# Input columns laid out by the host, scales spread by a product with ones, and a first unit whose weights come in row blocks

## The chip, the cores and the metric

The kernel runs on one core of one Trainium2 chip. The time is the device time of one execution in microseconds (us), and of several executions the median counts. The engines are TensorE (PE in the profile, with PEld for its weight loads), VectorE (DVE), ScalarE (ACT), GpSimd (POOL) and SyncE (SP), which only issues transfers here. Each engine works through its own instructions in order and waits at semaphores for the others.

## The reference

One decoder layer on 2048 tokens of 1024 float32 features. The part that the change touches is at the front: the tokens are normalised, multiplied by one large weight matrix, and three groups of four attention heads are cut out of the product.

```python
h = rms_norm(x, norm_w[layer])          # x * rsqrt(mean(x*x) + eps) * norm_w, per token
proj = h @ w_in[layer]                  # 1024 -> 9224 columns
(dn_qkv, dn_z, dn_b, dn_a, swa_q, swa_k, swa_v, swa_z, gates) = jnp.split(proj, split_points, axis=-1)
...                                     # branch A: a chunked gated delta rule
sq = partial_rope(rms_norm(grp(swa_q), q_norm_w[layer][:, None, :]), cos, sin)
sk = partial_rope(rms_norm(grp(swa_k), k_norm_w[layer][:, None, :]), cos, sin)
...                                     # branch B: windowed attention per group and head, merged by softmax sums
x = x + merged @ w_out[layer]
```

All of it is computed in float32 accuracy. Each large product is therefore made of three: both factors are split into a rounded part and the rest, and high by high, high by low and low by high are added up.

## The kernel before, in words

**The normalised input.** The tokens are worked in 16 tiles of 128. The products need a tile with the features on the partitions, so `hh` (rounded part) and `hl` (rest) hold it in 8 blocks of 128 features, in two halves of 4. For each tile t, `x_load` (L95) brings 128 x 1024 inputs, `x_norm` makes the sum of squares on ScalarE (L102) and the scale on GpSimd (L103, and L105 with a power of -1/2), and VectorE multiplies the tile by scale and norm weights in one instruction of 1024 elements (L106). `x_trans` then has TensorE transpose the 8 blocks (L116, products with an identity) into PSUM, from which ScalarE rounds each half into `hh` (L119) and VectorE subtracts it into `hl` (L120).

**The first stage** (`swa`, from the start to about 1044 us) is 12 units, one per head and group, of 16 steps. Step t of a unit multiplies token tile t by 384 weight columns (q, k and v of the head): 24 products of 384 columns (`s_proj`, L176 to L178), two blocks of features at a time, with slots between them. In the slots stand the pieces of an attention tile that is two steps older (`att_slots`): slot 0 transposes its probabilities (L265), slot 1 makes its scores (L249 to L251, VectorE's masking and row maximum L253 and L256, ScalarE's exponential L258), slot 2 multiplies by v (L273, L274) and transposes the q and k of the next one (L231, with L238 and L239 behind it). At the end of a step `s_norm` normalises q and k: ScalarE squares and sums (L191) and copies v (L192), GpSimd makes the scales (L195, L197), VectorE multiplies (L199), and GpSimd rotates (L207 to L210).

**Only in the first unit** are the token tiles made as well: in step t, after slot 1, `x_trans(t + 1)` and `x_norm(t + 2)`. The other units find them ready.

**Weights.** `w384` loads the 1024 x 384 weights of a unit in six pieces (four feature blocks by one of q, k, v; L155), and splits each with ScalarE (L79) and VectorE or GpSimd (L80). For the first unit this stands ahead of step 0; the second unit's pieces are split in steps 14 and 15 of the first, those of the later units one per step from step 6.

**What sets the order.** In this stage the order on TensorE, ScalarE, VectorE and GpSimd is the order in which the code is written; a scheduler places only the transfers, all on the SP queue. A tile of a pool with two or three buffers waits until the reader of an earlier one is done. PSUM has three `mm`, two `tp`, two `sc` and one `po`. After the first stage come the delta rule, its scan, and the last products, which the change leaves as they are.

## Time and profile before

| | us |
|---|---|
| median of 3 runs | 2417.84 |
| lowest, highest | 2412.42, 2421.81 |
| the profiled execution, its own time | 2415.66 |
| its span, first to last instruction | 2413.5 |
| TensorE busy in the span | 2362.7 |
| VectorE, ScalarE, GpSimd busy | 1160.2, 846.1, 835.1 |
| ScalarE's first square (L191) of tile 0 in unit 0 | 26.61 |
| the same of tile 15 in unit 0 | 126.35 |
| the same of tile 0 in unit 1 | 135.32 |

The profiled execution lies 2.18 us under the median of the runs, and 2.16 us of its time lie outside the span. In a row of the timeline stand the start, the duration (for a row that merges several instructions, from the first start to the last end), the engine, the source line, the operation, the tiles written and read, the sizes and the count; in brackets how long the engine had been idle before, and what released it. A matmul's row is longer than its share of the engine, because the next one starts while it drains: the distance of two starts is what one costs.

### The profile page before, as it was taken

To read this page: it belongs to the slowest core of one execution; us is meant where nothing else is said; L and a number is where in the kernel's file an instruction comes from. 1 tells how busy PE (TensorE), PEld (TensorE's weight loads), DVE (VectorE), ACT (ScalarE), POOL (GpSimd) and SP (SyncE) were. 2 spreads that over 40 slices of the span, in tenths; PEclk is the share of its full clock that TensorE was granted. 3 is DMA by queue.
4 is the path that set the end of the run, shared out by engine and by line. 5 is a ranking of instruction groups with operands and counts; after the bars stand their busy time and mean duration, and the time that the engine had idled before them with its cause. 6 is when DMAs were issued, how large, how long until landed. Compare 5 with 4: busy or idle time off the path is not lost.

```text
span 2413.5 us, 40161 instructions
## 1 busy us (share of the span) xinstructions
PE 2362.7 (98%) x13710; PEld 2147.6 (89%) x13710; DVE 1160.2 (48%) x2738; ACT 846.1 (35%) x2985; POOL 835.1 (35%) x1785
## 2 busy tenths in 40 slices
PE   7999999999999999999999999999999999999999
PEld 6999999999999999987777878888888878889998
DVE  4644433243344334343766665999444433454431
ACT  4544443244444333323665662111243313111110
POOL 3533433533343344410533551111133212442441
PEclk9999999999999999999999999999999999999999
DMA  4211101233343344433444443222566655555542
GB/s 139 72 44 35 39 23 50 87 113 97 100 118 104 100 120 115 115 98 101 124 122 120 111 120 114 75 75 71 180 200 192 185 165 156 162 181 157 150 139 75
DMA packets 348819, 274.22 MB, mean 114 GB/s; under 512 B 57864, under 2 KB 317256, under 8 KB 348232
## 3 DMA queue, kind: packets, MB, share of 16 engines
q1 hardware_dynamic: 348616, 271.66, 39.1%
q8 instruction: 109, 1.79, 0.3%
q14 instruction: 94, 0.77, 0.1%
HBM read 167.47 MB, written 104.10 MB: 113 GB/s over the span
## 4 chain that ended last, share of the span: by engine, by line
PE 86%; DMA 4%; DVE 4%; ACT 2%; POOL 2%; issue 1%; SPq 1%; DVEq 0%; ACTq 0%; POOLq 0%
PE mm L176 11%; PE mm L178 11%; PE mm L177 11%; PE mm L413 9%; PE mm L415 8%; PE mm L414 8%; PE mm L903 2%; PE mm L905 2%; PE mm L904 2%; PE mm L886 2%; PE mm L888 2%; PE mm L887 2%; DMA gcb<-gcscr 2%; PE po L274 2%; PE tp L231 2%; PE tp L265 1%
## 5 line engine op out<-in xcount | busy, mean ns | idle before, releaser
L176 PE MATMUL mm<-wh,hh 128*128 128x384 f32 (+1 forms) x1536 | 554.5, 361 | 2.4 <-ACT wh L79 2.4
L177 PE MATMUL mm<-wl,hh 128*128 128x384 f32 (+1 forms) x1536 | 519.4, 338 | 1.8 <-DVE wl L80 1.2
L178 PE MATMUL mm<-wh,hl 128*128 128x384 f32 (+1 forms) x1536 | 520.0, 339 | 0.0
L413 PE MATMUL mm<-hh,wh 128*128 128x512 f32 x1152 | 467.1, 406 | 0.0
L415 PE MATMUL mm<-hh,wl 128*128 128x512 f32 x1152 | 456.0, 396 | 0.0
L414 PE MATMUL mm<-hl,wh 128*128 128x512 f32 x1152 | 452.9, 393 | 0.0
L176 PEld LDWEIGHTS mm<-wh,hh 128*128 128x128 f32 x1536 | 290.4, 189 | 5.3 <-ACT wh L79 3.0
L177 PEld LDWEIGHTS mm<-wl,hh 128*128 128x128 f32 x1536 | 291.3, 190 | 2.5 <-DVE wl L80 1.4
L178 PEld LDWEIGHTS mm<-wh,hl 128*128 128x128 f32 x1536 | 289.7, 189 | 0.0
L415 PEld LDWEIGHTS mm<-hh,wl 128*128 128x128 f32 x1152 | 217.8, 189 | 47.7
L413 PEld LDWEIGHTS mm<-hh,wh 128*128 128x128 f32 x1152 | 217.9, 189 | 43.6
L414 PEld LDWEIGHTS mm<-hl,wh 128*128 128x128 f32 x1152 | 218.1, 189 | 41.9
L80 POOL TENSOR_TENSOR wl<-raw,wh 128x512 fp32r<-128x512 f32 (+1 forms) x75 | 106.9, 1437 | 405.4 <-ACT wh L79 405.0
L199 DVE SCALAR_TENSOR_TENSOR rec<-mm,st,wqk 128x128 f32<-128x128 f32 x256 | 78.1, 347 | 275.2 <-POOL st L197 261.6
L258 ACT ACTIVATE p<-sc,ol 128x128 f32<-128x128 f32 (+1 forms) x192 | 82.0, 427 | 342.8 <-DVE ol L256 310.2
L195 POOL TENSOR_SCALAR st<-st 128x2 f32<-128x2 f32 x192 | 48.8, 254 | 398.1 <-ACT rec L191 269.2
L886 PE MATMUL mm<-oh,hh 128*128 128x256 f32 x512 | 143.7, 281 | 3.0 <-DVE gt L890 2.9
L888 PE MATMUL mm<-oh,hl 128*128 128x256 f32 x512 | 142.9, 279 | 0.0
L887 PE MATMUL mm<-ol,hh 128*128 128x256 f32 x512 | 142.8, 279 | 0.0
L518 DVE SCALAR_TENSOR_TENSOR acc<-xr,cw,acc 128x512 f32<-128x512 f32 x144 | 121.8, 846 | 42.4 <-ACT acc L516 37.8
L197 POOL TENSOR_TENSOR st<-st,mhalf 128x2 f32<-128x2 f32 x192 | 134.7, 702 | 16.0
L191 ACT ACTIVATE rec<-mm 128x128 f32<-128x128 f32 x256 | 68.5, 273 | 160.6 <-PE mm L178 116.1
(240 smaller groups left out, 4346.6 us busy)
## 6 DMA issues: line engine op xcount, KB each, us to landing
raw<-in_w_in_dram SPq DMA_DIRECT2D x144, 256.0 KB, 3.1
rscr<-rec SPq DMA_DIRECT2D x128, 192.0 KB, 1.9
qk<-rscr SPq DMA_DIRECT2D x128, 128.0 KB, 2.3
gscr<-gt SPq DMA_DIRECT2D x64, 256.0 KB, 2.5
gt<-gscr SPq DMA_DIRECT2D x64, 256.0 KB, 3.4
oscr<-ol SPq DMA_DIRECT2D x192, 65.0 KB, 1.9
oc<-oscr SPq DMA_DIRECT2D x16, 780.0 KB, 5.0
rec<-rec SPq DMA_DIRECT2D x16, 768.0 KB, 5.3
```

The costliest lines, as they stand in the source:

```text
L80: eng.tensor_tensor(out=l, in0=raw, in1=h.bitcast(F32), op=ALU.subtract)
L176: nc.tensor.matmul(pr[:, :w], a, wh[:, k, :w], start=(k == 0), stop=False)
L177: nc.tensor.matmul(pr[:, :w], a, wl[:, k, :w], start=False, stop=False)
L178: nc.tensor.matmul(pr[:, :w], b, wh[:, k, :w], start=False, stop=(k == KT - 1))
L197: nc.gpsimd.tensor_tensor(out=st[:, 2:4], in0=st[:, 0:2], in1=self.mhalf[:, 0:2], op=ALU.pow)
L413: nc.tensor.matmul(pr, wh[:, k, :], a, start=(k == 0), stop=False)
L414: nc.tensor.matmul(pr, wh[:, k, :], b, start=False, stop=False)
L415: nc.tensor.matmul(pr, wl[:, k, :], a, start=False, stop=(k == KT - 1))
L518: nc.vector.scalar_tensor_tensor(out=acc, in0=xr[:, j:j + 512], scalar=w[:, j:j + 1], in1=acc, op0=ALU.mult, op1=ALU.add)
L886: nc.tensor.matmul(o, self.wbh[:, k, ms], oh[:, k, :], start=(k == b * 4), stop=False)
L887: nc.tensor.matmul(o, self.wbh[:, k, ms], ol[:, k, :], start=False, stop=False)
L888: nc.tensor.matmul(o, self.wbl[:, k, ms], oh[:, k, :], start=False, stop=(k == b * 4 + 3))
```

## The change

**The input, twice.** The host adds `xcol`, the same inputs with the features of each block on the partitions, and the norm weights as a 128 x 8 table `nwc`. For each token tile both forms are loaded (`x_load`), 512 KB each. The row form is only squared and summed (`x_stat`); GpSimd makes the scale as before and one instruction more, the identity times the scale, a diagonal `dg` of 128 x 128.

**The scale as a row.** `x_rows` multiplies 128 x 128 ones by that diagonal, so that each of 128 rows in PSUM holds the scales of the 128 tokens. `x_scale` multiplies the 8 blocks of `xc` in place, each by its norm weights (a scalar per partition) and by that row: 8 VectorE instructions of 128 elements. `x_high` rounds each half on ScalarE, `x_low` subtracts, the first half on VectorE and the second on GpSimd. The 8 transposes of a tile are gone, and the two PSUM tiles of `mm` that they took; the row takes a `tp`.

**When.** `XCOL` lists which tiles are made in which step of the first unit: one per step, two in steps 4 and 8, the last in step 12. The second unit's weights begin at step 13 with one piece split there, three in step 14 and two in step 15.

**The start.** The first unit's weights come in 8 row blocks of 128 features by q, k and v (`w_first`, 192 KB each), five ahead of the loop, split one by one in turn on VectorE and GpSimd. The transfers of the first `xcol` tile, the identity and the norm weights are issued by ScalarE. 24 products of 256 columns on the zeroed `kq` tile stand first on TensorE (`warm`).

```diff
--- before.py
+++ after.py
@@ -33,6 +33,8 @@
 C_SV = C_SK + 1536
 C_SZ = C_SV + 1536
 C_GT = C_SZ + 512
+
+XCOL = [[1], [2], [3], [4], [5, 6], [7], [8], [9], [10, 11], [12], [13], [14], [15], [], [], []]
 
 
 def dr(ap, off, dims):
@@ -83,42 +85,60 @@
     def x_setup(self, xp):
         nc = self.nc
         self.xp = xp
-        self.xt, self.xn = {}, {}
-        self.x_load(0)
-        self.nwb = xp.tile([P, D], F32, name="nwb", bufs=1)
-        nc.sync.dma_start(self.nwb, dr(self.i["norm_w"], 0, [[0, P], [1, D]]))
-        nc.sync.dma_start(self.ident, self.i["ident"])
-        self.x_norm(0)
-
-    def x_load(self, t):
+        self.xt, self.xc, self.dg = {}, {}, {}
+        self.ones = xp.tile([P, P], F32, name="ones", bufs=1)
+        self.nw = xp.tile([P, KT], F32, name="nw", bufs=1)
+        nc.vector.memset(self.ones, 1.0)
+        self.x_load(0, nc.scalar)
+        nc.scalar.dma_start(self.ident, self.i["ident"])
+        nc.scalar.dma_start(self.nw, self.i["nwc"])
+
+    def x_load(self, t, q=None):
+        nc = self.nc
         self.xt[t] = self.xp.tile([P, D], F32, name="xt", bufs=2)
-        self.nc.sync.dma_start(self.xt[t], dr(self.i["x"], P * t * D, [[D, P], [1, D]]))
-
-    def x_norm(self, t):
+        nc.sync.dma_start(self.xt[t], dr(self.i["x"], P * t * D, [[D, P], [1, D]]))
+        self.xc[t] = self.xp.tile([P, KT, P], F32, name="xc", bufs=2)
+        (q or nc.sync).dma_start(self.xc[t].rearrange("p k c -> p (k c)"), dr(self.i["xcol"], P * t * D, [[D, P], [1, D]]))
+
+    def x_stat(self, t):
         nc = self.nc
         xt = self.xt.pop(t)
         st = self.xp.tile([P, 2], F32, name="xst", bufs=2)
-        xn = self.xn[t] = self.xp.tile([P, D], F32, name="xn", bufs=2)
-        nc.scalar.activation(xn, xt, AF.Square, accum_out=st[:, 0:1])
+        dg = self.dg[t] = self.xp.tile([P, P], F32, name="dg", bufs=2)
+        nc.scalar.activation(xt, xt, AF.Square, accum_out=st[:, 0:1])
         nc.gpsimd.tensor_scalar(out=st[:, 0:1], in0=st[:, 0:1], scalar1=1.0 / D, scalar2=EPS,
                                 op0=ALU.mult, op1=ALU.add)
         nc.gpsimd.tensor_tensor(out=st[:, 1:2], in0=st[:, 0:1], in1=self.mhalf[:, 0:1], op=ALU.pow)
-        nc.vector.scalar_tensor_tensor(out=xn, in0=xt, scalar=st[:, 1:2], in1=self.nwb, op0=ALU.mult, op1=ALU.mult)
-
-    def x_trans(self, t):
-        nc = self.nc
-        xn = self.xn.pop(t)
-        n, c = t // 4, (t % 4) * P
+        nc.gpsimd.tensor_scalar(out=dg, in0=self.ident, scalar1=st[:, 1:2], scalar2=None, op0=ALU.mult)
+
+    def x_rows(self, t):
+        pt = self.ps.tile([P, 512], F32, name="tp", bufs=2)
+        self.nc.tensor.matmul(pt[:, :P], self.ones, self.dg.pop(t), start=True, stop=True)
+        return pt[:, :P]
+
+    def x_scale(self, t, rows, half):
+        xc = self.xc[t]
+        for k in range(half * 4, half * 4 + 4):
+            self.nc.vector.scalar_tensor_tensor(out=xc[:, k, :], in0=xc[:, k, :], scalar=self.nw[:, k:k + 1], in1=rows,
+                                                op0=ALU.mult, op1=ALU.mult)
+
+    def x_high(self, t, half):
+        n, c, ks = t // 4, (t % 4) * P, slice(half * 4, half * 4 + 4)
+        self.nc.scalar.activation(self.hh[:, n, ks, c:c + P], self.xc[t][:, ks, :], AF.Copy)
+
+    def x_low(self, t, half, eng):
+        n, c, ks = t // 4, (t % 4) * P, slice(half * 4, half * 4 + 4)
+        eng.tensor_tensor(out=self.hl[:, n, ks, c:c + P], in0=self.xc[t][:, ks, :], in1=self.hhf[:, n, ks, c:c + P],
+                          op=ALU.subtract)
+
+    def x_col(self, t):
+        rows = self.x_rows(t)
         for half in range(2):
-            pt = self.ps.tile([P, 512], F32, name="mm", bufs=3)
-            for j in range(4):
-                k = half * 4 + j
-                nc.tensor.transpose(pt[:, j * P:(j + 1) * P], xn[:, k * P:(k + 1) * P], self.ident)
-            ks = slice(half * 4, half * 4 + 4)
-            src = pt.rearrange("p (k c) -> p k c", c=P)
-            nc.scalar.activation(self.hh[:, n, ks, c:c + P], src, AF.Copy)
-            nc.vector.tensor_tensor(out=self.hl[:, n, ks, c:c + P], in0=src, in1=self.hhf[:, n, ks, c:c + P],
-                                    op=ALU.subtract)
+            self.x_scale(t, rows, half)
+        for half in range(2):
+            self.x_high(t, half)
+            self.x_low(t, half, (self.nc.vector, self.nc.gpsimd)[half])
+        self.xc.pop(t)
 
 
     def swa_setup(self, sp):
@@ -131,6 +151,34 @@
         self.rope = sp.tile([P, 16, 32], F32, name="rope", bufs=1)
         self.att = []
         self.att_next = 0
+
+    def warm(self, count):
+        pr = self.ps.tile([P, 512], F32, name="mm", bufs=3)
+        for _ in range(count):
+            self.nc.tensor.matmul(pr[:, :256], self.kq[:, 0, 0, :], self.kq[:, 0, 0:2, :].rearrange("p a c -> p (a c)"),
+                                  start=True, stop=True)
+
+    def w_first(self, wp, h, g):
+        nc, i = self.nc, self.i
+        wh = wp[0].tile([P, KT, wp[1]], F32R, name="wh")
+        wl = wp[0].tile([P, KT, wp[1]], F32R, name="wl")
+        self.wqk = self.sp.tile([P, 2, P], F32, name="wqk", bufs=1)
+        raws = []
+
+        def load():
+            k = len(raws)
+            raw = self.rawp.tile([P, 4, P], F32, name="raw")[:, 0:3, :] if k % 5 < 3 else \
+                self.xp.tile([P, 3, P], F32, name="raw0", bufs=2)
+            nc.sync.dma_start(raw, dr(i["w_in"], k * P * NIN + C_SQ + g * 512 + h * P, [[NIN, P], [1536, 3], [1, P]]))
+            raws.append(raw.rearrange("p a c -> p (a c)"))
+
+        def high(k):
+            nc.scalar.activation(wh[:, k, :384], raws[k], AF.Copy)
+
+        def low(k):
+            (nc.gpsimd if k % 2 else nc.vector).tensor_tensor(out=wl[:, k, :384], in0=raws[k],
+                                                              in1=wh[:, k, :384].bitcast(F32), op=ALU.subtract)
+        return (wh, wl, self.wqk), load, high, low
 
     def w384(self, wp, h, g, first=False):
         nc, i = self.nc, self.i
@@ -310,43 +358,66 @@
         nc = self.nc
         step = self.step
         nu = len(units)
-        gen = self.w384(wps[0](), *units[0], first=True)
-        w = {0: next(gen)}
-        for _ in range(3):
-            next(gen)
+        w0, load, high, low = self.w_first(wps[0](), *units[0])
+        w = {0: w0}
+        for _ in range(5):
+            load()
+        self.warm(24)
+        self.x_stat(0)
+        rows = self.x_rows(0)
+        high(0)
+        low(0)
+        self.x_scale(0, rows, 0)
+        high(1)
+        low(1)
+        high(2)
+        self.x_high(0, 0)
+        self.x_scale(0, rows, 1)
+        self.x_low(0, 0, nc.vector)
+        self.x_high(0, 1)
+        self.x_low(0, 1, nc.gpsimd)
+        self.xc.pop(0)
+        low(2)
         self.x_load(1)
+        for k in range(3, 8):
+            if k < 6:
+                load()
+            high(k)
+            low(k)
+            if k == 4:
+                self.x_stat(1)
+        self.x_load(2)
+        for j, nm in enumerate(("q_norm_w", "k_norm_w")):
+            nc.sync.dma_start(w0[2][:, j, :], dr(self.i[nm], units[0][1] * P, [[0, P], [1, P]]))
         nc.sync.dma_start(self.rope, self.i["rope"])
         nc.sync.dma_start(self.mask, self.i["mask"])
-        self.x_trans(0)
-        for _ in gen:
-            pass
-        self.x_norm(1)
         for u in range(nu):
             gen = None
             for t in range(16):
-                if u == 0 and t + 2 < 16:
-                    self.x_load(t + 2)
                 s = dict(h=units[u][0], g=units[u][1], t=t, pr=None, w=w[u])
                 self.s_proj(s, (0, 1))
                 self.att_slots(step, 0)
                 self.s_proj(s, (2, 3))
                 self.att_slots(step, 1)
-                if u == 0 and t < 15:
-                    self.x_trans(t + 1)
-                    if t < 14:
-                        self.x_norm(t + 2)
-                    else:
+                if u == 0:
+                    for c in XCOL[t]:
+                        self.x_col(c)
+                        if c + 2 < 16:
+                            self.x_load(c + 2)
+                        if c + 1 < 16:
+                            self.x_stat(c + 1)
+                    if t == 12:
                         xctx.close()
                 self.s_proj(s, (4, 5))
                 self.att_slots(step, 2)
                 self.s_proj(s, (6, 7))
                 self.s_norm(s)
                 self.att_add(s, step)
-                if u + 1 < nu and t >= (14 if u == 0 else 6):
+                if u + 1 < nu and t >= (13 if u == 0 else 6):
                     if gen is None:
                         gen = self.w384(wps[(u + 1) % 2](), *units[u + 1])
                         w[u + 1] = next(gen)
-                    for _ in range(4 if u == 0 else 1):
+                    for _ in range((2, 3, 3)[t - 13] if u == 0 else 1):
                         next(gen, None)
                 step += 1
         self.step = step
@@ -1048,6 +1119,8 @@
     nc = bacc.Bacc("TRN2", target_bir_lowering=False, num_devices=1)
     data = {name: np.ascontiguousarray(inputs[name]) for name in _INS}
     data.update(consts())
+    data["xcol"] = np.ascontiguousarray(data["x"].reshape(16, P, KT, P).transpose(0, 3, 2, 1)).reshape(T, D)
+    data["nwc"] = np.ascontiguousarray(data["norm_w"].reshape(KT, P).T)
     arrays, ins = {}, {}
     for name, a in data.items():
         arrays[f"in_{name}_dram"] = a
```

The order of VectorE's instructions in a step of the first unit, before, from one subtraction of the k and q tile to the next (`kq` and `qk` are the attention's, `sc` and `ol` the score and its maximum, `xn` and `hl` the token tile):

```order
L239 TENSOR_TENSOR kq<-tp,kq 128x256
L199 SCALAR_TENSOR_TENSOR qk<-mm,st,wqk 128x128 x2
L253 ISA sc,ol<-sc,mask 128x256
L253 ISA ol 128x1
L256 TENSOR_SCALAR ol<-ol 128x1
L120 TENSOR_TENSOR hl<-mm,hh 128x4x128 x2
L106 SCALAR_TENSOR_TENSOR xn<-xt,xst,nwb 128x1024
L276 COPY ol<-po 128x128
```

And now, in the same place (lines are those of the changed kernel; `xc` is the token tile):

```order
L287 TENSOR_TENSOR kq<-tp,kq 128x256
L247 SCALAR_TENSOR_TENSOR qk<-mm,st,wqk 128x128 x2
L301 ISA sc,ol<-sc,mask 128x256
L301 ISA ol 128x1
L304 TENSOR_SCALAR ol<-ol 128x1
L122 SCALAR_TENSOR_TENSOR xc<-xc,nw,tp 128x128 x8
L131 TENSOR_TENSOR hl<-xc,hh 128x4x128
L324 COPY ol<-po 128x128
```

Eight small instructions on `xc` stand where two subtractions and one long multiplication stood; the q and k scaling and the score are still ahead of them.

GpSimd in a step of the first unit, before (`xst` is the token scale, `st` that of q and k):

```order
L103 TENSOR_SCALAR xst<-xst 128x1
L105 TENSOR_TENSOR xst<-xst,mhalf 128x1
L195 TENSOR_SCALAR st<-st 128x2
L197 TENSOR_TENSOR st<-st,mhalf 128x2
L207 TENSOR_TENSOR t_696<-qk,rope 128x64
L208 TENSOR_TENSOR t_697<-qk,rope 128x64
```

And now:

```order
L131 TENSOR_TENSOR hl<-xc,hh 128x4x128
L109 TENSOR_SCALAR xst<-xst 128x1
L111 TENSOR_TENSOR xst<-xst,mhalf 128x1
L112 TENSOR_SCALAR dg<-ident,xst 128x128
L243 TENSOR_SCALAR st<-st 128x2
L245 TENSOR_TENSOR st<-st,mhalf 128x2
```

The subtraction of the second half and the diagonal are new, and both stand ahead of the scale of q and k.

TensorE in step 9 of the first unit, from the scores (L297 to L299 now) over the row of scales to the next products:

```order
L298 MATMUL sc<-kq 128x256
L299 MATMUL sc<-kq 128x256
L116 MATMUL tp<-dg,ones 128x128
L224 MATMUL mm<-wh,hh 128x384
L225 MATMUL mm<-wl,hh 128x384
```

One product stands where `L116 MATMUL mm<-ident,xn 128x128 x8` stood. Behind the first unit the order of all five queues is what it was.

## The prediction

> **What bounds the kernel now.** I read the page's first part, then the busy time by stretches, then the timeline of the first unit, one engine after another. The change only touches what stands ahead of the second unit, so one view decides: where TensorE idles there.
>
> ```profile
> PE 2362.7 (98%) x13710; PEld 2147.6 (89%) x13710; DVE 1160.2 (48%) x2738; ACT 846.1 (35%) x2985; POOL 835.1 (35%) x1785
> 0.00:30.00 30.00, 15.03 (x63) 13.52 (x64) 10.87 (x16) 11.97 (x24) 6.75 (x18) 1.00 0.68 204
> 60.00:90.00 30.00, 29.32 (x189) 26.82 (x188) 19.05 (x48) 16.19 (x54) 16.11 (x36) 1.00 0.31 85
> 150.00:180.00 30.00, 30.00 (x194) 29.79 (x193) 11.08 (x38) 12.71 (x54) 10.76 (x32) 1.00 0.09 24
> ```
> ```profile
> 26.61 0.28 ACT L191 ACTIVATE qk<-mm 128x128 f32<-128x128 f32 x1 [1.49 <-PE mm L178]
> 106.81 0.28 ACT L191 ACTIVATE qk<-mm 128x128 f32<-128x128 f32 x1 [0.17 <-PE mm L178]
> 126.35 0.28 ACT L191 ACTIVATE qk<-mm 128x128 f32<-128x128 f32 x1
> 135.32 0.28 ACT L191 ACTIVATE qk<-mm 128x128 f32<-128x128 f32 x1 [1.31 <-PE mm L178]
> 140.78 0.28 ACT L191 ACTIVATE qk<-mm 128x128 f32<-128x128 f32 x1 [0.68 <-PE mm L178]
> 61.23 1.32 PE L116 MATMUL mm<-ident,xn 128*128 128x128 f32 x8
> 62.30 0.42 PE L176 MATMUL mm<-wh,hh 128*128 128x384 f32 x1
> 68.12 1.32 PE L116 MATMUL mm<-ident,xn 128*128 128x128 f32 x8
> ```
>
> TensorE has 15 us of idle time in the first 30 us; from 60 us on it is full (29.3 of 30), while VectorE and GpSimd are at 64% and 54% there. The first square (L191) marks the end of a step's products: tiles 0, 12 and 15 of the first unit, then tiles 0 and 1 of the second. A step of the first unit takes 68.12 - 61.23 = 6.9 us, one of the second 140.78 - 135.32 = 5.45 us; the difference of 1.45 is the eight transposes (1.07 from 61.23 to 62.30, the rest around them). Between the units stand 8.97 us, 3.5 more than a step. So three things can be won: the start, 1.45 us a step, and the 3.5 us. My landmark is 135.32: behind it nothing changes its order, and what the landmark moves, the end moves.
>
> **The change part by part.** *On TensorE* the eight transposes go and one product of ones comes. Its nearest row is a float32 product of 128 columns, also shown as x2:
>
> ```profile
> 193.19 0.39 PE L274 MATMUL po<-v,pT 128*128 128x128 f32 x2
> 193.41 0.38 PE L231 MATMUL tp<-ident,qk 128*128 128x128 f32 x2
> ```
>
> It costs 0.22, with the switch about 0.36. If TensorE stayed the bound, a step would take 5.45 + 0.36 = 5.8 us. It will not stay, because of what the others get.
>
> *The loop from tile to tile.* VectorE's order is: scale of q and k (waits for GpSimd), score, then the eight small multiplications. ScalarE then rounds the second half, GpSimd subtracts it, and only behind that, in its own order, makes the next token scale, the diagonal, and the scale of q and k for which VectorE waits. So the multiplications of one tile lead to those of the next through three engines, whatever TensorE does. Rows for each link:
>
> ```profile
> 1787.52 0.61 DVE L748 SCALAR_TENSOR_TENSOR S<-S,eglb,po 128x128 f32<-128x128 f32 x2 [1.61 <-PE po L746]
> 68.06 0.61 DVE L199 SCALAR_TENSOR_TENSOR qk<-mm,st,wqk 128x128 f32<-128x128 f32 x2 [0.34 <-POOL st L197]
> 68.59 0.42 DVE L253 CUSTOM_DVE_ANT_0 sc<-sc,mask 128x256 f32<-128x256 f32 x1
> 69.11 0.15 DVE L256 TENSOR_SCALAR ol<-ol 128x1 f32<-128x1 f32 x1
> 8.41 0.63 ACT L79 ACTIVATE wh<-raw 128x512 fp32r<-128x512 f32 x1 [3.00 <-DMA raw<-in_w_in_dram]
> 63.81 1.07 ACT L102 ACTIVATE xn<-xt 128x1024 f32<-128x1024 f32 x1
> 65.83 0.20 ACT L191 ACTIVATION_READ_ACCUMULATOR qk<-mm 128x1 f32 x1
> 11.52 1.26 POOL L80 TENSOR_TENSOR wl<-raw,wh 128x512 fp32r<-128x512 f32 x1 [1.12 <-ACT wh L79]
> 65.05 0.19 POOL L103 TENSOR_SCALAR xst<-xst 128x1 f32<-128x1 f32 x1 [2.06 <-ACT xn L102]
> 65.33 0.55 POOL L105 TENSOR_TENSOR xst<-xst,mhalf 128x1 f32<-128x1 f32 x1
> 27.33 0.19 POOL L195 TENSOR_SCALAR st<-st 128x2 f32<-128x2 f32 x1 [1.29 <-ACT qk L191]
> 27.60 0.70 POOL L197 TENSOR_TENSOR st<-st,mhalf 128x2 f32<-128x2 f32 x1
> L680 POOL MEMSET S<- 128x128 f32 x4 | 0.6, 204 | 0.0
> L892 POOL TENSOR_TENSOR gt<-gt 128x256 f32<-128x256 f32 x64 | 48.3, 754 | 141.4 <-DVE gt L890 141.1
> ```
>
> - Eight multiplications: L748 has their form (a tile times a scalar times PSUM, in place). Two take 0.61, so 0.35 for the last and 0.265 a step: 7 x 0.265 + 0.345 = 2.20.
> - Rounding 512 values out of SBUF: L79, 0.63, and 0.04 to get there: 0.67.
> - GpSimd's subtraction: as L80, 1.26, and 0.09 to start: 1.35.
> - Token scale: 65.05 to 65.88, 0.83.
> - The diagonal has no row. Below it lies the write of as many values (0.20), above it half way between 0.19 and the two-tensor 256 columns (0.75), 0.47. I take 0.32, nearer the middle, and 0.08 of waiting for the power: 0.40.
> - Scale of q and k: 27.33 to 28.30, 0.97.
> - VectorE's two q and k products: 0.04 and 0.53 until the score begins: 0.57.
> - Score to the end of its maximum (68.59 to 69.26): 0.67.
>
> The sum is 7.66 us for one tile. ScalarE's own branch (square to last accumulator, 63.81 to 66.03, 2.2) is shorter than GpSimd's 1.35 + 0.83 + 0.40 = 2.6 beside it, and covered. In steps 4 and 8 a second tile follows without q, k and score: 2.20 + 0.67 + 1.35 + 0.83 + 0.40 and 0.48 for its row: 5.93. So TensorE, which needs 5.8 a step, waits 1.9 us in each, mostly for the k and q tile and for the diagonal, and about 5 us for the second diagonal in steps 4 and 8. The gain per step becomes a loss of 0.76.
>
> The old row of L195 in this stretch is longer, because VectorE's 1024-element multiplication held GpSimd:
>
> ```profile
> 66.12 1.12 POOL L195 TENSOR_SCALAR st<-st 128x2 f32<-128x2 f32 x1 [0.25 <-ACT qk L191]
> ```
>
> That instruction is gone, and in the new order VectorE stands waiting at that moment, so I take the free 0.97. The Trainium skill (SBUF — State Buffer, section "SBUF: two separate sides") has it that VectorE with two SBUF inputs and GpSimd exclude each other for a whole instruction, which the 1.12 against 0.19 bears out; by it the first half's subtraction on VectorE could hold the second half's on GpSimd.
>
> *The transfers* double to 1 MB a tile, 137 GB/s at 7.66 us, where more was moved:
>
> ```profile
> xt<-in_x_dram SPq DMA_DIRECT2D x16, 512.0 KB, 3.5
> 5.00:10.00 5.00, 1.97 (x8) 1.57 (x8) 1.30 (x2) 1.73 (x5) 1.63 (x3) 1.00 0.97 264
> 4.26 1.06 ACT L102 ACTIVATE xn<-xt 128x1024 f32<-128x1024 f32 x1 [2.27 <-DMA xt<-in_x_dram]
> ```
>
> A tile's columns are requested when those two tiles older have been subtracted, 4.2 us into their loop, and needed two loops (15.3) after its start: 11 us for a landing of 3.5, even with SP's output transfers ahead. Nothing, unless landing takes over 11.
>
> *The start.* The first tile landed at 4.26. Now both forms go ahead of all else: later by 0 at best, by 0.52 MB / 264 GB/s = 2.0 at worst; I take 1.0, so 5.2. Square 1.15, token scale 0.83 and waits: 7.3; diagonal 7.7; row at half clock 8.3; multiplications 10.5; rounding and subtraction 12.5; one weight block on GpSimd (384 of 512 columns of 1.26) 13.5; tile 1's scale and diagonal 14.7; its row 15.2, multiplications 17.4; the loop to the q and k products, 22.1. That is where tile 2's multiplications start.
>
> *The sum to the landmark.* Tile 3: 22.1 + 7.66 - 0.67 (no score yet) = 29.1. From there to tile 15 ten loops and two short ones: 29.1 + 76.6 + 11.9 = 117.6. Its row was done about 1.8 earlier; TensorE then has half a step left (2.9), so tile 12's square stands at 118.8, against 106.81. Three free steps of 5.45: 135.2. Then the second unit: 5.45 and a stall. Before it was 3.5 with three pieces to split behind step 15; now two stay, and one would expect 0 to 3.5; I take 1.5. That gives 142.1.
>
> *The clock.* Products were at half speed early, and again after a stall:
>
> ```profile
> 24.86 0.52 PE L178 MATMUL mm<-wh,hl 128*128 128x384 f32 x1
> 25.18 0.52 PE L176 MATMUL mm<-wh,hh 128*128 128x384 f32 x1
> 25.89 0.34 PE L176 MATMUL mm<-wh,hh 128*128 128x384 f32 x1
> 26.06 0.34 PE L177 MATMUL mm<-wl,hh 128*128 128x384 f32 x1
> 130.00:132.00 2.00, 1.21 (x5) 1.21 (x6) 1.29 (x5) 0.56 (x2) 0.97 (x3) 0.85 0.80 192
> 132.00:134.00 2.00, 2.00 (x10) 2.00 (x10) 0.29 (x1) 0.37 (x1) 0.00 (x0) 0.50 0.71 202
> ```
>
> Starts lie 0.32 apart up to 25.2 and 0.17 from 25.9 on; after gaps between 128 and 131 us the granted clock fell to 0.50. The 24 products on zeros, some 5 us at half speed, end near 7, and TensorE then mostly waits until about 10; I credit them with nothing. Waits of 5 us in steps 4 and 8 should bring the half clock back; most of it falls into slack, and I add 1.0 (0 to 3). The Trainium skill (TensorE: Matmul & The Clock Gate, section "What's actually happening") gives half rate after an idle window of about 3.4 us; the trace shows it after shorter gaps. By that rule alone only the two long waits would cost, at most 1.7 each, an estimate from that page.
>
> So the landmark goes from 135.32 to 143.1, +7.8. On the profiled execution's 2415.66 that is 2423.5; the median of the runs stands 2.2 above it, so I say 2425. A difference under 0.5%, 12.1 us, can't be told from no change here: this forecast is "no change", on its slow side.
>
> **The rivals.**
> *The loop doesn't close* and TensorE stays the bound. It would need GpSimd's scale of q and k ready before VectorE asks. Steps 1 to 12 at 5.8 with two more rows: tile 12's square at about 23 + 11 x 5.8 + 0.7 = 87.5, the landmark at 87.5 + 16.35 + 5.45 + 1.5 = 110.8, so 24.5 us less: 2393. For it: in the old order TensorE was the bound at 64% of VectorE. Against it: the queues are in order, and every link has a row.
> *GpSimd is held inside the loop*, slower than before. If its subtraction or scale runs beside a VectorE instruction that holds it, as in the 1.12 row, each loop costs up to 0.93 more; over 13 loops 12 us: 2437. It decides "slower" from 0.33 a loop on (the 4.3 us that 7.8 lacks to 12.1). For it: VectorE's first-half subtraction (as long as L79's 0.63) ends just as GpSimd's begins. Against: the scale's moment is free.
> *The warm products hold the clock*: step 0's 24 products would save 24 x 0.15 = 3.6 us of TensorE, nearly all under the loop of tile 1; 1 us, within the first case.
>
> **How the numbers follow.** The loop as computed 0.60, GpSimd held (or the loop longer by another of its links) 0.28, TensorE the bound 0.12. The forecast's own range: diagonal -1.7 to +1.0, GpSimd's subtraction 0 to +2.5, start -1 to +1, stall -1.5 to +2, clock -1 to +2: 2419 to 2433. To leave out no more than 2 in 10 I stretch it to both rivals, without the whole of the fast one: 2408 to 2438. Faster 0.12, same 0.59, slower 0.29.
>
> **What would show it.** In the changed kernel's timeline: the first multiplication of a token tile every 7.7 us in steps 5 to 12, GpSimd's subtraction directly behind ScalarE's rounding and its scale of q and k directly ahead of VectorE's products; TensorE at about 75% from 30 to 115 us, waiting for the diagonal; tile 12's square at 119 and the landmark at 143. A step under 6.9 us would prove the loop wrong, transfers ending VectorE's waits would prove the cover wrong, and a landmark moved by another amount than the end would put something behind the second unit.

## The result, and the profile after

The median goes from 2417.84 us to 2431.17 (nine runs of each), a ratio of 1.0053 with a 95% interval from 1.0041 to 1.0065: a little slower. The profiled execution took 2432.58 us, its span 2430.5, 17.0 more than before; tile 0 of the second unit moved from 135.32 to 151.79, by 16.5. What moves this landmark moves the end.

The first line of the page after, then the busy time by stretches (columns: length, busy time of TensorE, its loads, VectorE, ScalarE, GpSimd, granted clock, share and rate of the transfers):

```profile
PE 2363.4 (97%) x13638; PEld 2144.4 (88%) x13638; DVE 1164.5 (48%) x2835; ACT 850.5 (35%) x2987; POOL 855.9 (35%) x1819
```
```profile
0.00:30.00 30.00, 22.36 (x90) 19.31 (x90) 12.18 (x36) 14.43 (x33) 15.07 (x28) 0.83 0.81 259
60.00:90.00 30.00, 22.06 (x127) 19.08 (x125) 16.86 (x63) 14.30 (x47) 17.05 (x38) 0.99 0.42 147
150.00:180.00 30.00, 30.00 (x194) 29.78 (x194) 10.44 (x37) 11.79 (x52) 10.33 (x32) 1.00 0.10 28
```

From 60 to 90 us TensorE was busy 29.3 of 30 us before and is now 22.1; no other engine is above 17.1. An idle bottleneck with nobody full is the picture of a loop. The first squares of tiles 0, 12 and 15 of the first unit and of tile 0 of the second, from the timeline of ScalarE:

```profile
21.64 0.26 ACT L239 ACTIVATE qk<-mm 128x128 f32<-128x128 f32 x1
129.94 0.27 ACT L239 ACTIVATE qk<-mm 128x128 f32<-128x128 f32 x1
145.10 0.28 ACT L239 ACTIVATE qk<-mm 128x128 f32<-128x128 f32 x1
151.79 0.28 ACT L239 ACTIVATE qk<-mm 128x128 f32<-128x128 f32 x1 [0.68 <-PE mm L226]
```

The start gained 5.0 us (26.61 to 21.64); by tile 12 it is a loss of 23.1 (106.81 to 129.94); behind step 12, without tiles to make, 6.7 come back. One loop in the middle, VectorE's and GpSimd's rows:

```profile
63.53 2.16 DVE L122 SCALAR_TENSOR_TENSOR xc<-xc,nw,tp 128x128 f32<-128x128 f32 x8
70.47 0.61 DVE L247 SCALAR_TENSOR_TENSOR qk<-mm,st,wqk 128x128 f32<-128x128 f32 x2 [2.35 <-POOL st L245]
71.00 0.43 DVE L301 CUSTOM_DVE_ANT_0 sc<-sc,mask 128x256 f32<-128x256 f32 x1
71.60 2.16 DVE L122 SCALAR_TENSOR_TENSOR xc<-xc,nw,tp 128x128 f32<-128x128 f32 x8
```
```profile
66.44 1.30 POOL L131 TENSOR_TENSOR hl<-xc,hh 128x512 fp32r<-128x512 f32 x1 [2.19 <-ACT hh L127]
67.82 0.19 POOL L109 TENSOR_SCALAR xst<-xst 128x1 f32<-128x1 f32 x1
68.09 0.55 POOL L111 TENSOR_TENSOR xst<-xst,mhalf 128x1 f32<-128x1 f32 x1
68.74 0.61 POOL L112 TENSOR_SCALAR dg<-ident,xst 128x128 f32<-128x128 f32 x1
69.43 0.19 POOL L243 TENSOR_SCALAR st<-st 128x2 f32<-128x2 f32 x1
69.71 0.73 POOL L245 TENSOR_TENSOR st<-st,mhalf 128x2 f32<-128x2 f32 x1
```

VectorE starts the next tile 8.07 us after the last. GpSimd works from 66.44 to 70.44 without a gap over 0.1, and VectorE's products of q and k start 0.03 behind it. The view of waits, first 150 us, names the links (sum, times, longest):

```profile
DVE qk L247 <- POOL st L245: 37.9, 16, 4.2
POOL hl L131 <- ACT hh L127: 37.2, 16, 3.8
ACT hh L127 <- DVE xc L122: 31.2, 32, 4.1
PE tp L116 <- POOL dg L112: 24.7, 14, 7.5
```

### The profile page after: what moved, and what is told of

It is laid out like the page before. It is cut to its first block, busy times and chain, and to the rows that moved or that the text cites. A ratio compares the mean times of both kernels' runs of the same rounds, so it can differ in the third digit from the quotient of the medians.

```text
span 2430.5 us, 40228 instructions
## 1 busy us (share of the span) xinstructions
PE 2363.4 (97%) x13638; PEld 2144.4 (88%) x13638; DVE 1164.5 (48%) x2835; ACT 850.5 (35%) x2987; POOL 855.9 (35%) x1819
## 4 chain that ended last, share of the span: by engine, by line
PE 84%; DVE 5%; DMA 4%; POOL 3%; ACT 2%; issue 2%; SPq 0%; POOLq 0%; DVEq 0%; ACTq 0%
PE mm L224 10%; PE mm L226 10%; PE mm L225 10%; PE mm L484 9%; PE mm L486 9%; PE mm L485 9%; PE mm L974 2%; PE mm L976 2%; PE mm L975 2%; PE mm L957 2%; PE mm L959 2%; PE mm L958 2%; DMA gcb<-gcscr 2%; PE po L322 2%; PE tp L279 2%
## 5 line engine op out<-in xcount | busy, mean ns | idle before, releaser
L243 POOL TENSOR_SCALAR st<-st 128x2 f32<-128x2 f32 x192 | 36.9, 192 | 390.7 <-ACT rec L239 268.0
```

## The experiments

Eleven runs were made, the last of them of a kernel that had run before. "Landmark" is ScalarE's first square of tile 0 of the second unit; a step or loop is read from start to start of VectorE's eight multiplications. Single runs are set beside the change's profiled 2432.58; the change's own runs lie between 2426.3 and 2433.4.

**The diagonal twice.**

```diff
         nc.gpsimd.tensor_scalar(out=dg, in0=self.ident, scalar1=st[:, 1:2], scalar2=None, op0=ALU.mult)
+        nc.gpsimd.tensor_scalar(out=dg, in0=self.ident, scalar1=st[:, 1:2], scalar2=None, op0=ALU.mult)
```

> The changed kernel, with GpSimd's diagonal instruction issued twice for every token tile (the second writes the same values again). Theory, the loop from tile to tile: GpSimd's second diagonal lies in every loop and costs its row in the trace of the change, from the diagonal's start to the next instruction's, 69.43 - 68.74 = 0.69 us. So a loop of 8.06 becomes 8.75, the second tile of a double step 6.67 becomes 7.36, and with 16 tiles the first square of the second unit moves from 151.8 to about 162.8; the execution becomes about 11 us longer than the change's 2432.6, near 2443.6. Rival, TensorE or its clock sets the step: GpSimd has slack, the loop stays at 8.06 and the end moves by 0 to 1 us. Rival, the doubled transfers set the step: the same, 0 to 1 us.

Of its timeline, two starts of multiplications and the landmark:

```profile
68.97 2.16 DVE L123 SCALAR_TENSOR_TENSOR xc<-xc,nw,tp 128x128 f32<-128x128 f32 x8
77.74 2.16 DVE L123 SCALAR_TENSOR_TENSOR xc<-xc,nw,tp 128x128 f32<-128x128 f32 x8
162.61 0.28 ACT L240 ACTIVATE qk<-mm 128x128 f32<-128x128 f32 x1 [0.68 <-PE mm L227]
```

The loop is 8.77, the landmark 162.61, the time 2442.78: 0.70 more a loop and 10.8 at the landmark. GpSimd has no slack in this loop although it is busy 17 of 30 us there.

**The new transfers left out from the third tile on,** 14 of 16; the products are then those of other inputs.

```diff
-        self.xt, self.xc, self.dg = {}, {}, {}
+        self.xt, self.xc, self.dg, self.xo = {}, {}, {}, {}
...
-        self.xc[t] = self.xp.tile([P, KT, P], F32, name="xc", bufs=2)
+        if t > 1:
+            self.xc[t] = self.xo[t % 2]
+            return
+        self.xc[t] = self.xo[t] = self.xp.tile([P, KT, P], F32, name="xc", bufs=2)
```

> The changed kernel, in which the columns of the inputs are loaded for token tiles 0 and 1 only; later tiles multiply the same two buffers again, so the products are those of other inputs, and 14 of the 16 new transfers of 512 KB are left out. Theory, the loop from tile to tile through VectorE, ScalarE and GpSimd: transfers have no part in it, the loop stays at 8.06 us (within 0.1), the first square of the second unit at 151.8 (within 1.5, some of it at the start), the total within 3 us of the change's 2432.6. Rival, the doubled transfers set the step: with half of them gone a step falls toward what TensorE needs, 5.8 to 6.9 us, and the first square of the second unit comes 12 us or more earlier. Rival, transfers slow the engines' accesses: single links of the loop get shorter by a tenth or more, the loop by 0.3 us or more.

Its busy time from 60 to 90 us, and two starts from its timeline:

```profile
60.00:90.00 30.00, 21.95 (x127) 18.98 (x125) 17.18 (x62) 14.68 (x47) 16.66 (x38) 0.94 0.24 76
```
```profile
63.10 2.15 DVE L125 SCALAR_TENSOR_TENSOR xc<-xc,nw,tp 128x128 f32<-128x128 f32 x8
71.14 2.15 DVE L125 SCALAR_TENSOR_TENSOR xc<-xc,nw,tp 128x128 f32<-128x128 f32 x8
```

76 GB/s instead of 147, and the loop is 8.04; landmark 150.88, time 2431.62. The transfers have no part in it.

**Without the products on zeros.**

```diff
-        self.warm(24)
```

> The changed kernel without the 24 products on zeros. Theory: they end before the first real products, whose starts lay 0.32 us apart with them too, the half speed; taking them away changes the first square of the second unit (151.8) by less than 1 us either way, and the total by 0 to 1. Rival, they keep the granted clock from falling further or let it rise sooner: without them the first units of products stay at half speed longer and the first square of unit 0 comes later than 21.64 by 1 us or more. Rival, they hold the start up (they occupy TensorE until about 7.1): the first square of unit 0 comes earlier by 0.5 us or more.

The first square of unit 0 came at 21.28 (21.64 with them), the landmark at 151.13, the time was 2429.03. The 0.66 on the landmark is inside what was expected and inside what starts differ by (below), so they neither cost nor win anything that shows.

**The diagonal on ScalarE.** A one-part repair: it stands behind ScalarE's work on q, k and v.

```diff
-        nc.gpsimd.tensor_scalar(out=dg, in0=self.ident, scalar1=st[:, 1:2], scalar2=None, op0=ALU.mult)
+    def x_diag(self, t):
+        self.nc.scalar.activation(self.dg[t], self.ident, AF.Copy, scale=self.xs[t][:, 1:2])
...
                 self.s_norm(s)
+                if u == 0 and XCOL[t] and XCOL[t][-1] < 15:
+                    self.x_diag(XCOL[t][-1] + 1)
```

> The changed kernel with the diagonal made by ScalarE (a copy of the identity with the token scale) instead of GpSimd, behind ScalarE's work on q, k and v where the step makes one tile, at once where it makes two. Theory, the loop from tile to tile: GpSimd goes from the token scale to the scale of q and k directly, each loop of a single step loses 0.69 us (8.06 becomes 7.37), the loops of the double steps 0 to 0.5; the first square of the second unit comes about 8 us earlier (ten loops of 0.69 and something of the start), at 143 to 145, and the total falls to about 2424. Rival, the step is set by TensorE, its clock or the transfers: the loop stays at 8.06. Rival, ScalarE becomes the late one, since its diagonal stands ahead of the transposed probabilities: the loop loses less than 0.4 and the wait moves to ScalarE.

Rows of VectorE, GpSimd and ScalarE in one loop (the last start is cut off by the stretch asked for), and the landmark:

```profile
59.49 2.15 DVE L125 SCALAR_TENSOR_TENSOR xc<-xc,nw,tp 128x128 f32<-128x128 f32 x8
64.04 0.55 POOL L112 TENSOR_TENSOR xst<-xst,mhalf 128x1 f32<-128x1 f32 x1
64.62 0.40 ACT L115 ACTIVATE dg<-ident,xst 128x128 f32<-128x128 f32 x1 [0.31 <-POOL xst L112]
64.67 0.19 POOL L246 TENSOR_SCALAR st<-st 128x2 f32<-128x2 f32 x1
66.81 0.87 DVE L125 SCALAR_TENSOR_TENSOR xc<-xc,nw,tp 128x128 f32<-128x128 f32 x3
142.76 0.28 ACT L242 ACTIVATE qk<-mm 128x128 f32<-128x128 f32 x1 [0.68 <-PE mm L229]
```

The loop is 7.32, the landmark 142.76, the time 2420.96. 0.70 more a loop had moved the landmark by +10.8, 0.75 less moves it by -9.0: the loop through GpSimd is shown, and the rivals that blamed TensorE, its clock or the transfers have fallen.

**The token scale one tile ahead, behind the scale of q and k.** Two versions; the second leaves the second half's subtraction on GpSimd, so it lacks the edit of `x_low`. The loads and the second unit's weights follow (loads a tile or two earlier, the weights from step 14).

```diff
-XCOL = [[1], [2], [3], [4], [5, 6], [7], [8], [9], [10, 11], [12], [13], [14], [15], [], [], []]
+XCOL = [[t + 1] for t in range(15)] + [[]]
...
-            self.x_low(t, half, (self.nc.vector, self.nc.gpsimd)[half])
+            self.x_low(t, half, self.nc.vector)
...
-                        if c + 1 < 16:
-                            self.x_stat(c + 1)
...
                 self.s_norm(s)
+                if u == 0:
+                    for c in XCOL[t]:
+                        if c + 2 < 16:
+                            self.x_stat(c + 2)
```

> The changed kernel in another order: the square and sum, the token scale and the diagonal of a tile are made one tile ahead and behind the step's scale of q and k, so GpSimd does them after VectorE has been released; the second half's subtraction stands on VectorE like the first; one tile is made in each of steps 0 to 14, and the second unit's weights begin at step 14 as in the kernel before. Theory, the loop from tile to tile: GpSimd's links between ScalarE's rounding and the scale of q and k go (subtraction 1.38, token scale 0.92, diagonal 0.69 in the change's trace, 66.44 to 69.43), and what is left of the loop, 8.06 - 2.99 = 5.1 plus some 0.6 for VectorE's subtraction, is no longer than what TensorE needs; a step comes to about 6.1 us (TensorE's 5.8, an estimate in the prediction, or VectorE's own work). Tile 15's multiplications then stand near 24.5 + 13 x 6.1 = 104, the first square of the second unit, which is 3 + 6 + 9 later (half a step, step 15, the old stall), near 122 instead of 151.8 and 135.3 before, and the total near 2403, 0.6 per cent under the kernel before. Rival, the clock: if half speed after each wait, not the loop, makes the steps long, they stay above 7 us and the first square above 135. Rival, TensorE's order (row behind a diagonal that is now early) is no help since the q and k tile still waits: steps of 6.9, as before, and a total that differs from before by the start only, some 5 us less.

> As the kernel with the scale one tile ahead, but the second half's subtraction stays on GpSimd, ahead of its scale of q and k. Theory, the loop from tile to tile: it still closes over GpSimd, without token scale and diagonal: 8.06 less 67.82 to 69.43 of the change's trace, 1.61, gives 6.45 us a step. Tile 15's multiplications near 24.5 + 13 x 6.45 = 108, the first square of the second unit near 126, the total near 2407. Rival, the place of the subtraction does not matter (VectorE or TensorE sets the step): the same step as with both subtractions on VectorE, within 0.15 us.

The first version, its busy time from 60 to 90 us, then rows of its timeline: two starts of multiplications, GpSimd's diagonal between them, and the squares of tile 14 and of the second unit:

```profile
60.00:90.00 30.00, 29.41 (x186) 27.63 (x184) 25.58 (x86) 20.25 (x65) 16.70 (x45) 1.00 0.55 170
```
```profile
62.93 2.15 DVE L127 SCALAR_TENSOR_TENSOR xc<-xc,nw,tp 128x128 f32<-128x128 f32 x8
64.45 0.61 POOL L117 TENSOR_SCALAR dg<-ident,xst 128x128 f32<-128x128 f32 x1
68.97 2.15 DVE L127 SCALAR_TENSOR_TENSOR xc<-xc,nw,tp 128x128 f32<-128x128 f32 x8
102.17 0.27 ACT L244 ACTIVATE qk<-mm 128x128 f32<-128x128 f32 x1
115.33 0.28 ACT L244 ACTIVATE qk<-mm 128x128 f32<-128x128 f32 x1 [0.68 <-PE mm L231]
```

Steps of 6.04, TensorE busy 29.4 of 30 again, landmark 115.33, median 2394.09: 0.9909 of the kernel before (0.9894 to 0.9924). The diagonal costs the same 0.61, but beside other work. The landmark came 7 us sooner than expected: tile 2's multiplications started at 22.02 and not at 24.5, the first steps were shorter than 6.04 (first squares at 19.66, 24.75, 30.10), and the gap between the units was 7.4, not 9. Two starts of the second version:

```profile
62.74 2.16 DVE L127 SCALAR_TENSOR_TENSOR xc<-xc,nw,tp 128x128 f32<-128x128 f32 x8
69.19 2.16 DVE L127 SCALAR_TENSOR_TENSOR xc<-xc,nw,tp 128x128 f32<-128x128 f32 x8
```

It takes 6.45 a step, as expected; landmark 124.52, median 2403.88, ratio 0.9948 (0.9931 to 0.9965). So the token scale and the diagonal are worth 1.6 a step. Taking the subtraction off GpSimd as well is worth another 0.4, which is what is left until TensorE is nearly full.

**The start of the change alone**, token tiles 1 to 15 as before. In the second run (the second diff, against the first run) tile 1's square stands further ahead on ScalarE.

```diff
-                if u == 0:
-                    for c in XCOL[t]:
-                        self.x_col(c)
...
+                if u == 0 and t < 15:
+                    self.x_trans(t + 1)
+                    if t < 14:
+                        self.x_norm(t + 2)
```
```diff
         for k in range(3, 8):
...
             low(k)
+            if k == 4:
+                self.x_norm(1)
-        self.x_norm(1)
```

> The start of the change alone: token tile 0 comes as columns, with the row of scales, the first unit's weights in row blocks and the products on zeros; token tiles 1 to 15 are made as in the kernel before (eight transposes, row form alone), and the second unit's weights begin at step 14. Theory: the start is worth what the first square shows, 26.61 before against 21.64 in the change, 5 us; the steps of 6.9 and the 9 us between the units come back, so the first square of the second unit is near 130.3 and the total near 2411. Rival, the start's gain is lost in the next steps, because tile 1 is late (in the change its multiplications came at 17.9 and steps 1 to 3 took 7.5 to 7.9): the first square of the second unit at 133 or more. Rival, the start has no gain of its own without the new tiles: 135.

> The start of the change alone once more, token tiles 1 to 15 as before, but tile 1's square and sum stand on ScalarE behind the fifth weight block, where the change has them, and no longer behind the eighth. In the run before, that square started at 19.94, after ScalarE had waited 5.7 us for the last weight block, and tile 1's transposes at 23.41; the first square of unit 0 came at 28.52. Theory, the start is worth its 5 us if tile 1 is not late: tile 1's square at about 13, its long multiplication at about 15 to 17, the first square of unit 0 at 21 to 23, that of the second unit 4 to 5.5 us under the 135.3 of the kernel before, the total 4 to 5 us less. Rival, the transfers of the first 20 us bind: the norm weights as rows (512 KB) and the last weight blocks still come late, the first square stays above 25, and the total within 2 us of the kernel before; then the start needs the column form of the other tiles too.

Of the first run, ScalarE's and TensorE's rows:

```profile
19.51 0.52 ACT L204 ACTIVATE wh<-raw 128x384 fp32r<-128x384 f32 x1 [5.71 <-DMA raw<-in_w_in_dram]
19.94 1.04 ACT L121 ACTIVATE xn<-xt 128x1024 f32<-128x1024 f32 x1
23.41 1.97 PE L135 MATMUL mm<-ident,xn 128*128 128x128 f32 x8 [7.67 <-DVE xn L125]
```

Tile 1 is queued behind a weight block that lands late: first square 28.52, landmark 137.31, median 2419.13, ratio 1.0012 (1.0003 to 1.0021), the expectation missed. With tile 1 ahead of it the first square is back at 21.65 and the landmark at 131.59, 3.7 under before; the median of 2414.67 gives 0.9988 (0.9979 to 0.9998), half of what was expected. The start is worth 4 to 5 us where it is measured; at the end 2.6 of it are left by the medians, and the interval leaves room for 0.5 to 5.

**The order of six products.** TensorE still waited 0.28 a step for the rest of the next tile. Here it comes two products later; first without the products on zeros, then with them, and beside that the first version again.

```diff
         for k in ks:
-            a, b = self.hh[:, t // 4, k, cs], self.hl[:, t // 4, k, cs]
+            a = self.hh[:, t // 4, k, cs]
             nc.tensor.matmul(pr[:, :w], a, wh[:, k, :w], start=(k == 0), stop=False)
             nc.tensor.matmul(pr[:, :w], a, wl[:, k, :w], start=False, stop=False)
+        for k in ks:
+            b = self.hl[:, t // 4, k, cs]
             nc.tensor.matmul(pr[:, :w], b, wh[:, k, :w], start=False, stop=(k == KT - 1))
```

> The kernel with the scale one tile ahead and both subtractions on VectorE, with two small edits: the six products of two feature blocks in the order rounded by both weights for either block, then the two with the rest, so that the rest is needed two products later; and without the products on zeros. Theory: in each step TensorE waits about 0.28 us for the first rest of the next tile (65.74 where 65.46 would follow, then 71.78 where 71.50 would), and two products of 0.17 ahead of it cover that, so a step falls from 6.04 to about 5.76 and 13 steps give 3.6 us; the start without the products on zeros gives 0.3 to 0.5; the first square of the second unit at about 111.5 instead of 115.33, the total near 2390. Rival, the loop over VectorE, ScalarE and GpSimd sets the 6.04 and the wait of TensorE only fills it up: steps stay within 0.05 of 6.04, and the total within 1 us.

> The kernel with the scale one tile ahead and the six products of two blocks in the new order, now with the 24 products on zeros again. In the run without them the steps fell from 6.04 to 5.855 us, but the start lost as much (half speed until 22.8 instead of 16.4), and the first square of the second unit stood at 116.14. Theory, the products on zeros bring full speed sooner: the start is as in the first kernel of this order (full speed near 16), the steps 5.855, the first square of the second unit near 115.33 - 13 x 0.185 = 112.9, the total 2 to 3 us under that kernel. Rival, when full speed comes is not set by these products (the change without them had it at 14.9, with them at 20.8): it falls anywhere between 14 and 24, the first square of the second unit between 112 and 117, and the total is the same within 2 us.

> The kernel with the scale one tile ahead and both subtractions on VectorE, word for word as run before (2394.09), now beside the one with the new order of products, so that both stand against the same runs of the kernel before. Theory: 0.9909 of the kernel before again, within 0.9894 to 0.9924; steps of 6.04; the first square of the second unit at 115.3 if full speed comes near 16 again. Rival, the clock of the start varies from run to run: then this square differs from 115.33 by up to 3 us either way with the steps unchanged at 6.04.

Without the products on zeros: steps of 5.855, landmark 116.14, median 2397.55 (0.9921; 0.9906 to 0.9936). With them: steps of 5.855, landmark 114.72, median 2395.26 (0.9916; 0.9903 to 0.993). The first version beside it: steps of 6.04, landmark 116.28, median 2394.17 (0.9915; 0.9901 to 0.9928). The steps are shorter as expected, and the end is not earlier. The two runs gave it back in different places. Without the products on zeros it went at the start: the first square of unit 0 came at 22.17, in the two runs of the first version at 19.66 and 20.60. With them it went between the units: TensorE's rows, then the busy time of two microseconds:

```profile
108.95 0.44 PE L229 MATMUL mm<-wh,hh 128*128 128x384 f32 x1 [1.41 <-ACT wh L81]
110.22 0.69 PE L230 MATMUL mm<-wl,hh 128*128 128x384 f32 x1 [0.83 <-DVE wl L82]
```
```profile
110.00:112.00 2.00, 1.78 (x6) 1.78 (x7) 0.71 (x4) 0.57 (x2) 0.48 (x2) 0.54 0.99 270
```

TensorE waits for the second unit's weights and then works at a granted clock of 0.54: 8.95 from tile 15's square (105.77) to the landmark, 7.4 in the version with longer steps (108.88 to 116.28). The new order is not the reason: without the products on zeros it had gaps of 0.99 and 1.22 there, a clock of 1.00, and 7.4 as well. The version with the scale one tile ahead, at 2394, is the best found: 21 to 22 us under the kernel before, where the change lay 13 above it.

## Why the prediction was right, and where its sizes were off

- **The loop closes, and TensorE waits in it: right.** Every link stood where it was put; the doubled and the moved diagonal show that GpSimd's work is on the path. TensorE was busy 71% of the time from 30 to 115 us (predicted about 75%).
- **The loop of 7.66: 0.41 short.** From start to start the links measured 2.91 to GpSimd's subtraction (predicted 2.87), 1.38 (1.35), 0.92 for the token scale (0.83), 0.69 for the diagonal (0.40), 1.04 for the scale of q and k (0.97), 0.53 (0.57) and 0.60 (0.67). The mis-sized term is the diagonal: the instruction took 0.61, outside its bounds of 0.20 and 0.47. A write of constants and a product of two tensors did not bracket a product of one tensor with a scalar.
- **Steps 4 and 8: 0.74 short each.** The second tile followed after 6.67 (48.79 to 55.46), not 5.93: 0.29 from the diagonal, 0.09 from the token scale, and 0.33 from the row, which was made at half speed after TensorE had waited 7.5 us (predicted about 5).
- **The start: 3.25 short.** Tile 2's multiplications started at 25.35, not 22.1. The input landed 0.9 later (first square 6.07 against 5.2), three diagonals (tiles 0, 1 and 2) cost 0.3 more each, and GpSimd's chain ahead of tile 1's scale was slower than its free rows:

```profile
12.34 1.47 POOL L131 TENSOR_TENSOR hl<-xc,hh 128x512 fp32r<-128x512 f32 x1 [2.52 <-ACT hh L127]
13.13 1.10 DVE L179 TENSOR_TENSOR wl<-raw,wh 128x384 fp32r<-128x384 f32 x1 [0.46 <-ACT wh L176]
13.77 1.32 POOL L179 TENSOR_TENSOR wl<-raw,wh 128x384 fp32r<-128x384 f32 x1
15.18 0.43 POOL L109 TENSOR_SCALAR xst<-xst 128x1 f32<-128x1 f32 x1
```

  These share 12 to 15 us with VectorE's subtraction, which itself took 1.10 where it took 0.56 at 7.82. That is the rule that the prediction weighed, in the Trainium skill (SBUF — State Buffer, section "SBUF: two separate sides"); the trace agrees with it here, at the start. In the loop the second half's subtraction took 1.30, near the free 1.26, because VectorE's had ended at 66.29, so GpSimd was not held inside the loop. But that case was put together with "or the loop longer by another of its links", with "slower" from 0.33 a loop on, and this second half is what came: 0.41, most of it the diagonal.
- **The transfers: right**, by the run with half of them.
- **The products on zeros: right**, worth under 1 us at the landmark of the change (0.66). In the new order of products the two runs differ by 1.4 there, with one execution each.
- **The clock and the tail.** The waits of 7.5 brought half speed back, as foreseen. TensorE's row behind the first of them, and the busy time of its first two microseconds at the lower clock:

```profile
54.63 0.80 PE L116 MATMUL tp<-dg,ones 128*128 128x128 f32 x2 [7.54 <-POOL dg L112]
```
```profile
48.00:50.00 2.00, 0.00 (x0) 0.00 (x0) 1.97 (x10) 0.62 (x3) 1.06 (x4) 0.56 0.59 242
```

  From 48 to 59 us the granted clock was 0.53. The shorter waits of the single steps did not bring it down (0.99 from 60 to 90 us). The rule that the prediction took from the Trainium skill (TensorE: Matmul & The Clock Gate, section "What's actually happening"), half rate after an idle window of about 3.4 us, has the same waits cost and spare speed. The moment does not fit it: the clock fell near 48.2, about 1.2 us after the last product had ended at 47.09. Tile 15's multiplications to the landmark took 24.85, where the prediction had 25.5 with its 1.0 for the clock; the stall between the units was 6.69 - 5.45 = 1.24 (1.5).

Together, on the landmark: start 3.25, the loops 6.1 (two short ones 1.5 of it), tail -0.65, so 8.7 more than 7.8. The sign, the mechanism and the range held, the forecast "no change, on its slow side" only barely: the prediction had drawn its line at 0.5%, 12.1 us, and the median is 13.3 us up, with an interval of 0.41% to 0.65% on both sides of that line. The median was 6 us above the point, not 9, and the difference is luck of which executions were profiled: this one lies 1.4 above its median, that of before lay 2.2 under.

## What to carry to other kernels

Removing work from the busiest engine helps only as far as the loop of the others lets it: write down one round through all engines, in queue order, before counting what the busiest one saves. An instruction that is needed a step later does not belong ahead of the one for which another engine stands waiting; moving three such instructions behind it was worth 1.6 us a step here, more than the 1.45 of the eight transposes. An operation without a row should be bounded by rows of the same operand kinds; smaller and larger neighbours of other kinds did not hold it.

## What the runs showed of the hardware

- GpSimd's product of 128 x 128 float32 with a scalar per partition took 0.61 us, ScalarE's copy with a scale of the same tile 0.40 (0.31 to the next start).
- Full speed of TensorE at the start comes at different times, with and without products on zeros. TensorE's rows of the change (with them) and of the run without:

```profile
20.51 0.52 PE L224 MATMUL mm<-wh,hh 128*128 128x384 f32 x1
20.83 0.39 PE L225 MATMUL mm<-wl,hh 128*128 128x384 f32 x1
21.06 0.34 PE L226 MATMUL mm<-wh,hl 128*128 128x384 f32 x1
```
```profile
14.61 0.52 PE L224 MATMUL mm<-wh,hh 128*128 128x384 f32 x1
15.49 0.34 PE L226 MATMUL mm<-wh,hl 128*128 128x384 f32 x1
```

  Spacing falls from 0.32 to 0.17 us near 20.8 in the one and near 15.3 in the other; in the run with the new product order and without them it was near 22.8, and in the kernel before at 25.5. 5.5 us of products on zeros with a pause of 1.8 behind them did not settle it. The kernel that ran twice, the first version, reached it at 15.4 us in one execution and at 16.5 in the other, by the granted clock. (That column can't be read ahead of its first change: it gives 1.00 from 12 to 15 us for the run without products on zeros, whose products lie 0.32 apart there.) The Trainium skill (TensorE: Matmul & The Clock Gate, section "What's actually happening") has a window that runs freely and is not set back by the kernel, so that the moment varies by half a microsecond. The spread here is several us over the kernels above, and 1.1 in the one that ran twice.
- A wait that did not cost speed in one run did in another. Gaps between the units of 0.73 and 1.17 stayed at a granted clock of 1.00 in the first version; 0.56 and 1.17 in the kernel before were followed by 0.50, and 1.41 and 0.83 in the new order of products by 0.54. Why is open.
- Between the landmark and the end the profiled executions took from 2273.4 to 2281.5 us, so a gain of 3 us at the front can't be told from none at the end of one execution (the early-tile start: 3.7 less at the landmark, 0.4 less in its span, 2.6 less in its median).
